# A hybrid SSD and attention layer in exact float32: parameters loaded behind the first block, x turned in the middle of a step, the last step in two banks

## The chip, the core and the metric

One core of a Trainium2 chip runs the whole layer. Its engines work in their own orders and wait for one another by semaphores: TensorE (PE in the rows; PEld are its weight loads) multiplies and transposes, VectorE (DVE) and ScalarE (ACT) do elementwise work, GpSimd (POOL) builds masks, and SyncE (SP) issues most of the loads. The metric is device time in microseconds of one execution, the median of several runs.

## The reference

```python
def hybrid_layer(x, norm_w, w_in, conv_w, conv_b, dt_bias, a_log, d_skip, ssd_norm_w, w_out):
    h = rmsnorm(x, norm_w)
    proj = h @ w_in                       # (256, 2048) @ (2048, 13344)
    z, xbc, dt_raw, q, k, v, g = jnp.split(proj, IN_SPLITS, axis=-1)
    xbc = jax.nn.silu(causal_depthwise_conv(xbc, conv_w, conv_b))
    xs, bm, cm = jnp.split(xbc, ...)
    y = ssd_chunked_scan(xs, softplus(dt_raw + dt_bias), -exp(a_log), bm, cm) + d_skip * xs
    y_ssd = group_rmsnorm(y * silu(z)) * ssd_norm_w
    y_sba = stick_breaking_attention(q, k, v) * silu(g)
    return x + concatenate([y_ssd, y_sba]) @ w_out    # (256, 4096) @ (4096, 2048)
```

A final RMSNorm with final_norm_w closes it. There are 256 tokens, all data are float32, and the time goes into the two large products.

## The kernel before

**Products.** Each large product is done in blocks of 256 or 512 columns of the weights, and a block in steps of two slices (kind "tok", the tokens' activations stand in the array) or four (kind "feat") of 128 rows of the weights. To keep float32 accuracy, weights and activations are each split into a high part that TensorE multiplies in one pass and a low part, and three products are added: high by high, high by low, low by high. `load` (L190) brings weights from HBM into one of four raw buffers; `cut` (L205) makes the parts, the high one as a cast on ScalarE (L218) and the low one as a subtraction on VectorE (L221); `product` (L224) issues the matmuls, for a "tok" step 12 of 512 columns (L235 to L237: two slices, two blocks of 128 tokens, three products).

**The first block, z0** (L282 to L306), is written out by hand for TensorE, ScalarE and VectorE. Here x arrives too: `load_x` (L352) loads 256 columns of x between the weight loads, on SP's queue; `prep_x` (L356) transposes them on TensorE (L363, four transposes a step), ScalarE scales each by norm_w into hT's high part (L366) and VectorE makes the low part (L367). The loop runs prep_x(s), then the cut of step s, then the product of step s-1. Eight matmuls of the identity (L296) go ahead, and norm_w itself comes through a small load and one transpose (`load_rows`, L100).

**Later blocks** run z1 to z3, c0, c1 (C and dt), b0, b1 (B), x0 to x3, then q, k, v, g of four head groups, and the output blocks o0 to o3. Each step's `advance` cuts two steps ahead. Between steps, `drain` (L143) takes side work from queues in order, up to a budget per step; an item's `lag` holds its queue back for so many steps after it. Side work here is the scaling of h, the convolutions (`conv`, L429), `decays` (L536), `b_tok` (L503, transposes B), `cb_block` (L556, products of C and B), the scan and the attention. Tile's scheduler places it in each engine's order.

**Parameters.** Convolution weights, biases, ssd_norm_w and three per-head vectors are loaded by GpSimd's queue at the start (L91 to L107) and two of them turned in `row_scale_bc` (L381).

**The end.** In o3 the second block of 128 tokens trails the first by three steps. `fin_last` (L837) adds the accumulator to x in two pieces of 256 columns (L846), squares each on ScalarE (L820) with a sum, forms 1/sqrt of the mean (L850 to L856), scales (L860 to L865) and stores eight pieces.

## Time and profile before

| what | value |
|---|---|
| median of 3 runs | 837.83 us (837.17 to 838.25) |
| the profiled execution | 837.44 us |
| its span in the trace | 835.7 us |
| TensorE busy | 821.0 us, 98% |
| VectorE, ScalarE busy | 520.3 us, 448.0 us |
| loaded from HBM | 152.43 MB, 185 GB/s over the span |

The rows further down are from this execution; their times count from the start of its span. A matmul's record is longer than its distance to the next one, since matmuls are pipelined, so distances between starts tell the rate, and short pauses hide in the records. In square brackets behind a row stand the idle time of its engine before it and what ended that.

### The profile page before, as it was taken

What the parts mean: (1) busy time and instruction counts of PE and PEld (TensorE: products, weight loads), DVE (VectorE), ACT (ScalarE), POOL (GpSimd) and SP (SyncE); (2) the same over time, 40 slices, a digit from 0 to 9 for tenths busy, and PEclk for the clock granted to TensorE, in tenths of its full rate; (3) what the DMA queues carried; (4) which work ended last, traced back from release to release, by engine and by line L of the source; (5) the groups of instructions that cost most, each with busy time, mean ns of one, the idle gap of its engine ahead of it and who ended that gap; (6) DMA issues with size and microseconds to landing.
All of it is one profiled execution on the core that took longest, in us unless ns stands there. A gap on an engine that the chain in (4) does not pass through costs nothing.

```text
span 835.7 us, 11182 instructions
## 1 busy us (share of the span) xinstructions
PE 821.0 (98%) x4341; PEld 701.0 (84%) x4341; DVE 520.3 (62%) x712; ACT 448.0 (54%) x671; POOL 63.7 (8%) x131
## 2 busy tenths in 40 slices
PE   8999999999999999999999999999999999999995
PEld 6888898888888888888888888888888888888884
DVE  4664959678896867676545654466545655455543
ACT  4754648785676756375444543455444544344433
POOL 2000000200101010022000400022000310000000
PEclk9999999999999999999999999999999999999998
DMA  8756477646656556464566446654565846555712
GB/s 289 274 199 201 136 213 219 204 151 202 197 157 199 170 187 199 119 186 152 154 199 202 151 152 201 201 164 150 191 187 179 338 152 191 184 185 197 250 52 100
DMA packets 113990, 155.29 MB, mean 186 GB/s; under 512 B 2836, under 2 KB 78704, under 8 KB 113552
## 3 DMA queue, kind: packets, MB, share of 16 engines
q1 hardware_dynamic: 112416, 149.18, 56.4%
q0 software_dynamic: 1520, 5.40, 2.0%
q8 instruction: 34, 0.56, 0.3%
q14 instruction: 20, 0.16, 0.1%
HBM read 152.43 MB, written 2.13 MB: 185 GB/s over the span
## 4 chain that ended last, share of the span: by engine, by line
PE 92%; DVE 3%; ACT 2%; issue 1%; DMA 1%; POOL 0%; SPq 0%; ACTq 0%; POOLq 0%
PE mm_g L241 7%; PE mm_k L241 7%; PE mm_o L235 7%; PE mm_o L236 7%; PE mm_o L237 7%; PE mm_q L241 6%; PE mm_x L241 5%; PE mm_k L244 4%; PE mm_g L244 4%; PE mm_v L237 3%; PE mm_v L235 3%; PE mm_v L236 3%; PE mm_z L235 3%; PE mm_z L236 3%; PE mm_z L237 3%; PE mm_q L244 3%
## 5 line engine op out<-in xcount | busy, mean ns | idle before, releaser
L221 DVE TENSOR_TENSOR lo_o<-raw_o,hi_o 128x1024 fp32r<-128x1024 f32 x64 | 78.1, 1224 | 74.3 <-ACT hi_o L218 74.2
L218 ACT CAST hi_o<-raw_o 128x1024 fp32r<-128x1024 f32 x64 | 67.1, 1053 | 93.5 <-PE mm_o L237 80.0
L241 PE MATMUL mm_q<-hT,hi_q 128*128 128x512 f32 x256 | 82.0, 401 | 0.0
L241 PE MATMUL mm_x<-hT,hi_x 128*128 128x512 f32 x256 | 81.7, 400 | 0.0
L241 PE MATMUL mm_k<-hT,hi_k 128*128 128x512 f32 x256 | 81.5, 400 | 0.0
L241 PE MATMUL mm_g<-hT,hi_g 128*128 128x512 f32 x256 | 80.9, 397 | 0.0
L221 DVE TENSOR_TENSOR lo_g<-raw_g,hi_g 128x1024 fp32r<-128x1024 f32 x32 | 39.2, 1226 | 45.4 <-ACT hi_g L218 43.8
L221 DVE TENSOR_TENSOR lo_v<-raw_v,hi_v 128x1024 fp32r<-128x1024 f32 x32 | 39.2, 1224 | 39.9 <-ACT hi_v L218 38.4
L218 ACT CAST hi_g<-raw_g 128x1024 fp32r<-128x1024 f32 x32 | 33.7, 1052 | 51.5 <-PE mm_g L241 31.1
L218 ACT CAST hi_v<-raw_v 128x1024 fp32r<-128x1024 f32 x32 | 33.6, 1050 | 45.9 <-PE mm_v L237 24.2
L244 PEld LDWEIGHTS mm_k<-hT,lo_k 128*128 128x128 f32 x256 | 48.1, 188 | 11.4
L244 PEld LDWEIGHTS mm_g<-hT,lo_g 128*128 128x128 f32 x256 | 48.1, 188 | 11.3
L244 PEld LDWEIGHTS mm_q<-hT,lo_q 128*128 128x128 f32 x256 | 48.1, 188 | 11.3
L244 PEld LDWEIGHTS mm_x<-hT,lo_x 128*128 128x128 f32 x256 | 48.0, 188 | 11.3
L221 DVE TENSOR_TENSOR lo_k<-raw_k,hi_k 128x1024 fp32r<-128x1024 f32 x32 | 39.2, 1224 | 27.7 <-ACT hi_k L218 27.7
L221 DVE TENSOR_TENSOR lo_z<-raw_z,hi_z 128x1024 fp32r<-128x1024 f32 (+1 forms) x33 | 39.2, 1192 | 25.1 <-ACT hi_z L218 24.9
L221 DVE TENSOR_TENSOR lo_q<-raw_q,hi_q 128x1024 fp32r<-128x1024 f32 x32 | 40.1, 1253 | 23.6 <-ACT hi_q L218 19.0
L218 ACT CAST hi_q<-raw_q 128x1024 fp32r<-128x1024 f32 x32 | 33.5, 1047 | 37.8 <-PE mm_q L241 17.6
L235 PE MATMUL mm_z<-hi_z,hT 128*128 128x512 f32 x128 | 50.6, 396 | 0.0
L218 ACT CAST hi_k<-raw_k 128x1024 fp32r<-128x1024 f32 x32 | 33.5, 1048 | 31.6 <-PE mm_k L241 23.5
L244 PE MATMUL mm_x<-hT,lo_x 128*128 128x256 f32 x256 | 50.5, 278 | 0.0
L244 PE MATMUL mm_q<-hT,lo_q 128*128 128x256 f32 x256 | 50.5, 278 | 0.0
(247 smaller groups left out, 1984.3 us busy)
## 6 DMA issues: line engine op xcount, KB each, us to landing
raw_o<-in_w_out_dram SPq DMA_DIRECT2D x32, 1024.0 KB, 5.2
raw_x<-in_w_in_dram SPq DMA_DIRECT2D x16, 1024.0 KB, 5.3
raw_q<-in_w_in_dram SPq DMA_DIRECT2D x16, 1024.0 KB, 5.3
raw_k<-in_w_in_dram SPq DMA_DIRECT2D x16, 1024.0 KB, 5.4
raw_v<-in_w_in_dram SPq DMA_DIRECT2D x16, 1024.0 KB, 5.0
raw_g<-in_w_in_dram SPq DMA_DIRECT2D x16, 1024.0 KB, 5.3
raw_z<-in_w_in_dram SPq DMA_DIRECT2D x12, 1024.0 KB, 5.1
raw_b<-in_w_in_dram SPq DMA_DIRECT2D x4, 1024.0 KB, 5.4
```

Source lines behind the costliest of these rows:

```text
L218: ins = ac.copy(hi[:, ks, :], src[:, ks, :])
L221: ve.tensor_tensor(out=lo[:, ks, :], in0=src[:, ks, :], in1=hi[:, ks, :].bitcast(F32), op=ALU.subtract)
L235: te.matmul(o, lhsT=ah[:, ts], rhs=hi[:, k2, :], start=first, stop=False)
L236: te.matmul(o, lhsT=ah[:, ts], rhs=lo[:, k2, :], start=False, stop=False)
L237: te.matmul(o, lhsT=al[:, ts], rhs=hi[:, k2, :], start=False, stop=last)
L241: te.matmul(acc[i], lhsT=hi[:, k2, i * P:(i + 1) * P], rhs=hT[:, k, :, :].rearrange("p a s -> p (a s)"), start=first, stop=False, skip_gro ...
L244: te.matmul(acc[i][:, 0:SEQ], lhsT=lo[:, k2, i * P:(i + 1) * P], rhs=hT_hi[:, k, :], start=False, stop=last, skip_group_check=True)
```

## The change

Five edits. The parameters are loaded by SP's queue behind the loads that the first block issues, and turned eight steps after the evacuation of z0 (`load_params`, `turn_params`); norm_w is loaded by ScalarE's queue. In the first block a step's product is done in two halves of one slice, and the transposes of the next step's x stand between them; x is scaled (`scale_x`) ahead of the next step's cut, and in the first cut slice by slice. There are six matmuls of the identity instead of eight. The lag behind B's last convolution is four instead of three, with two more behind the last `b_tok`; and the last step of the trailing token block in o3 goes into two banks of 256 columns (`product_end`), whose second square is done by VectorE.

```diff
-    nc.sync.dma_start(out=nw_rows, in_=norm_w[0].rearrange("(k p) -> k p", p=P))
+    ac.dma_start(out=nw_rows, in_=norm_w[0].rearrange("(k p) -> k p", p=P))
...
+    def load_params():
+        nc.sync.dma_start(out=par[0:4 * NT, :], in_=conv_w[0].rearrange("j (n p) -> (j n) p", p=P))
+        nc.sync.dma_start(out=par[4 * NT:5 * NT, :], in_=conv_b[0].rearrange("(n p) -> n p", p=P))
+        nc.sync.dma_start(out=sn_rows, in_=ssd_norm_w[0].rearrange("(k p) -> k p", p=P))
+        for i, src in enumerate((dt_bias, a_log, d_skip)):
+            nc.sync.dma_start(out=heads_bc[:, i, :], in_=src[0].partition_broadcast(P))
...
-        parts = [slice(0, width)] if b is not blocks[0] or s else [slice(i, i + 1) for i in range(width)]
+        parts = [slice(0, width)] if each is None else [slice(i, i + 1) for i in range(width)]
         for ks in parts:
+            if each is not None:
+                each(ks.start)
             ins = ac.copy(hi[:, ks, :], src[:, ks, :])
...
+    def product_end(b, s, i, halves):
+
+        hi, lo = cuts[b["name"], s]
+        ts, width = slice(i * P, (i + 1) * P), KS[b["kind"]]
+        for h, o in enumerate(halves):
+            ns = slice(h * 256, (h + 1) * 256)
+            for k2 in range(width):
+                ah, al = b["acts"](s * width + k2)
+                te.matmul(o[:, 0:256], lhsT=ah[:, ts], rhs=hi[:, k2, ns], start=k2 == 0, stop=False)
+                te.matmul(o[:, 0:256], lhsT=ah[:, ts], rhs=lo[:, k2, ns], start=False, stop=False)
+                te.matmul(o[:, 0:256], lhsT=al[:, ts], rhs=hi[:, k2, ns], start=False, stop=k2 == width - 1)
...
-            for i in range(8):
+            for i in range(6):
                 te.matmul(warm[:, 0:P], lhsT=ident, rhs=ident, start=True, stop=True)
             load_rows(nwT, nw_rows, KIN, "ps_nw")
-            for s in range(KIN // 2 + 1):
-                if s == 0:
-                    advance(1)
-                if s < KIN // 2:
-                    prep_x(s)
-                    advance(s + 1)
-                if s > 0:
-                    product(b, s - 1, acc, range(NB))
-                    done += 1
+            turn_x(0)
+            advance(1, each=lambda i: scale_x(i))
+
+            for s in range(KIN // 2):
+                product(b, s, acc, range(NB), (0,))
+                if s + 1 < KIN // 2:
+                    turn_x(s + 1)
+                    for i in range(2):
+                        scale_x(2 * s + 2 + i)
+                    advance(s + 2)
+                product(b, s, acc, range(NB), (1,))
+                done += 1
+            load_params()
...
-            push(main, (0, 1.1), evac)
+            push(main, (0, 1.1), evac, lag=8)
+            push(main, (0.5, 0), turn_params)
...
-                push(main, (1.2, 0.8), lambda g=g: conv(ut[:, g, :], BN + g, BT[:, g, :]), lag=g // 3 * 3)
+                push(main, (1.2, 0.8), lambda g=g: conv(ut[:, g, :], BN + g, BT[:, g, :]), lag=g // 3 * 4)
...
-                push(main, (0, 0.2), lambda g=g: b_tok(g))
+                push(main, (0, 0.2), lambda g=g: b_tok(g), lag=g // 3 * 2)
...
+            ve.tensor_tensor(out=y[:, b, 1536:2048], in0=acc[0], in1=y[:, b, 1536:2048], op=ALU.add)
+            for i in range(2):
+                c0 = 1536 + i * 256
+                yi = y[:, b, c0:c0 + 256]
+                ve.tensor_tensor(out=yi, in0=acc[1 + i][:, 0:256], in1=yi, op=ALU.add)
+                if i == 0:
+                    square_y(b, c0, 256, 3)
+                else:
+                    junk = pools["fin"].tile([P, 256], F32, name="junk_y")
+                    ve.scalar_tensor_tensor(out=junk, in0=yi, scalar=1.0 / D_MODEL, in1=yi, op0=ALU.mult,
+                                            op1=ALU.mult, accum_out=ysq[:, b, 4:5])
```

**TensorE in the first block.** `ps_x_6` and `ps_x_7` are the transposes of x for step 3, `hi_z0_2` and `lo_z0_2` the parts of step 2's weights, `hi_z0_3` and `lo_z0_3` those of step 3. Before:

```order
L237 MATMUL mm_z0_138<-hi_z0_1_199,hT_111 128x512
L363 MATMUL ps_x_6_243<-ident_72,xt_1_116 128x128 x2
L363 MATMUL ps_x_7_248<-ident_72,xt_1_116 128x128 x2
L235 MATMUL mm_z0_138<-hi_z0_2_227,hT_111 128x512
L236 MATMUL mm_z0_138<-lo_z0_2_228,hT_111 128x512
L237 MATMUL mm_z0_138<-hi_z0_2_227,hT_111 128x512
```

In the changed kernel:

```order
L255 MATMUL mm_z0_132<-hi_z0_2_225,hT_105 128x512
L391 MATMUL ps_x_6_241<-ident_72,xt_1_110 128x128 x2
L391 MATMUL ps_x_7_244<-ident_72,xt_1_110 128x128 x2
L253 MATMUL mm_z0_132<-hi_z0_2_225,hT_105 128x512
L254 MATMUL mm_z0_132<-lo_z0_2_226,hT_105 128x512
L255 MATMUL mm_z0_132<-hi_z0_2_225,hT_105 128x512
L253 MATMUL mm_z0_132<-hi_z0_2_225,hT_105 128x512
L254 MATMUL mm_z0_132<-lo_z0_2_226,hT_105 128x512
L255 MATMUL mm_z0_132<-hi_z0_2_225,hT_105 128x512
L253 MATMUL mm_z0_132<-hi_z0_3_251,hT_105 128x512
L254 MATMUL mm_z0_132<-lo_z0_3_252,hT_105 128x512
```

The transposes for step 3 stood ahead of all 12 matmuls of step 2, which were followed by the transposes for step 4 and then step 3; now they stand behind the first six of step 2, and step 3 follows the other six.

**ScalarE at the same place**, in the changed kernel:

```order
L396 ACTIVATE hT_105<-ps_x_6_241,nwT_90 128x256
L396 ACTIVATE hT_105<-ps_x_7_244,nwT_90 128x256
L222 CAST hi_z0_3_251<-raw_z0_1_139 128x1024
L396 ACTIVATE hT_105<-ps_x_8_267,nwT_90 128x256
L396 ACTIVATE hT_105<-ps_x_9_270,nwT_90 128x256
L222 CAST hi_z0_4_279<-raw_z0_2_161 128x1024
```

From step 1 on this is the order of before, two scaled copies of x and then the cast of the same step; VectorE's is the same with its two low parts and the subtraction. In step 0 the two casts stood ahead of the copies, and now each stands behind one.

**TensorE at B's side products.** `ps_bt` are the transposes of B, `ps_cb` the products of C and B, `mm_x0_1` the block x0_1. Before:

```order
L244 MATMUL mm_x0_0_1398<-hT_111,lo_x0_0_3_1434 128x256 x2
L505 MATMUL ps_bt_0_1495<-ident_72,BT_124 128x128
L505 MATMUL ps_bt_1_1498<-ident_72,BT_124 128x128
L505 MATMUL ps_bt_2_1501<-ident_72,BT_124 128x128
L505 MATMUL ps_bt_3_1504<-ident_72,BT_124 128x128
L241 MATMUL mm_x0_1_1523<-hT_111,hi_x0_1_0_1455 128x512 x2
```

In the changed kernel:

```order
L262 MATMUL mm_x0_1_1497<-hT_105,lo_x0_1_0_1454 128x256 x2
L538 MATMUL ps_bt_0_1520<-ident_72,BT_118 128x128
L538 MATMUL ps_bt_1_1523<-ident_72,BT_118 128x128
L538 MATMUL ps_bt_2_1526<-ident_72,BT_118 128x128
L538 MATMUL ps_bt_3_1529<-ident_72,BT_118 128x128
L259 MATMUL mm_x0_1_1497<-hT_105,hi_x0_1_1_1473 128x512 x2
```

The transposes of B moved from ahead of the first step of x0_1 to behind it; the products of C and B, which stood within that first step, now stand between its third and fourth.

## Rows read from the trace of the kernel before

**Rows 1.** Page, busy times: engine, busy us (share of the span), instructions

```profile
PE 821.0 (98%) x4341; PEld 701.0 (84%) x4341; DVE 520.3 (62%) x712; ACT 448.0 (54%) x671; POOL 63.7 (8%) x131
```

**Rows 2.** Windows: stretch, its us, each engine's busy us (instructions), clock, DMA, GB/s

```profile
0.00:20.00 20.00, 16.18 (x76) 13.22 (x77) 8.72 (x15) 9.52 (x17) 4.82 (x17) 1.00 0.89 285
...
20.00:40.00 20.00, 20.00 (x94) 16.27 (x94) 13.02 (x17) 15.14 (x31) 0.00 (x0) 1.00 0.84 299
...
800.00:836.00 36.00, 26.55 (x118) 21.66 (x116) 13.34 (x25) 12.51 (x21) 0.00 (x0) 0.90 0.16 59
```

**Rows 3.** TensorE's waits: who waited for whom, us in total, times, longest

```profile
PE ps_x L363 <- DMA xt<-in_x_dram: 2.3, 2, 1.3
```

**Rows 4.** Timeline, a step of z0: start, us, engine, line, op [idle before it]

```profile
15.69 0.60 PE L363 MATMUL ps_x<-ident,xt 128*128 128x128 f32 x4
...
16.05 0.48 PE L235 MATMUL mm_z<-hi_z,hT 128*128 128x512 f32 x1
...
16.11 0.84 ACT L366 ACTIVATE hT<-ps_x,nwT 128x256 fp32r<-128x256 f32 x2 [1.38 <-PE ps_x L363]
...
16.36 0.40 PE L236 MATMUL mm_z<-lo_z,hT 128*128 128x512 f32 x1
...
16.84 1.04 ACT L218 CAST hi_z<-raw_z 128x1024 fp32r<-128x1024 f32 x1
...
17.92 1.23 DVE L221 TENSOR_TENSOR lo_z<-raw_z,hi_z 128x1024 fp32r<-128x1024 f32 x1 [0.42 <-ACT hi_z L218]
...
18.91 0.60 PE L363 MATMUL ps_x<-ident,xt 128*128 128x128 f32 x4
...
19.58 0.40 PE L236 MATMUL mm_z<-lo_z,hT 128*128 128x512 f32 x1
```

**Rows 5.** Timeline: transposes of steps 2 and 7, first matmul of z1

```profile
12.45 0.63 PE L363 MATMUL ps_x<-ident,xt 128*128 128x128 f32 x4 [1.32 <-DMA xt<-in_x_dram]
...
28.51 0.60 PE L363 MATMUL ps_x<-ident,xt 128*128 128x128 f32 x4
...
34.63 0.39 PE L235 MATMUL mm_z<-hi_z,hT 128*128 128x512 f32 x1
```

**Rows 6.** Timeline: the start, on SP's queue, TensorE and ScalarE

```profile
0.81 0.39 SPq L88 DMA_DIRECT2D nw_rows<-in_norm_w_dram  x1
...
5.46 1.11 PE L363 MATMUL ps_x<-ident,xt 128*128 128x128 f32 x4
...
5.49 0.62 ACT L218 CAST hi_z<-raw_z 128x512 fp32r<-128x512 f32 x1 [3.20 <-DMA raw_z<-in_w_in_dram]
...
7.55 0.63 PE L363 MATMUL ps_x<-ident,xt 128*128 128x128 f32 x4 [0.97 <-DMA xt<-in_x_dram]
```

**Rows 7.** Windows of one us in the first block

```profile
9.00:10.00 1.00, 1.00 (x6) 0.82 (x5) 0.69 (x2) 0.82 (x1) 0.00 (x0) 1.00 1.16 185
...
13.00:14.00 1.00, 1.00 (x6) 0.81 (x5) 0.60 (x2) 1.00 (x3) 0.00 (x0) 1.00 1.06 385
```

**Rows 8.** Timeline: B's side products on TensorE

```profile
160.94 0.33 PE L505 MATMUL ps_bt<-ident,BT 128*128 128x128 f32 x1 [0.37 <-ACT BT L439]
...
163.75 2.05 PE L560 MATMUL ps_cb<-CT,BT 128*128 128x128 f32 x16 [0.61 <-ACT Btok L506]
```

**Rows 9.** Timeline: matmuls of 256 columns; VectorE behind the last matmul

```profile
400.32 0.40 PE L244 MATMUL mm_k<-hT,lo_k 128*128 128x256 f32 x2
...
400.55 0.63 PE L241 MATMUL mm_k<-hT,hi_k 128*128 128x512 f32 x2
...
825.31 0.75 DVE L860 SCALAR_TENSOR_TENSOR yfw<-yfw,sums 128x512 f32<-128x512 f32 x1
...
826.59 0.76 DVE L846 TENSOR_TENSOR yfw<-mm_o,yfw 128x256 f32<-128x256 f32 x2 [0.54 <-PE mm_o L237]
...
827.99 0.22 DVE L850 SCALAR_TENSOR_TENSOR sums<-ysq,sums 128x1 f32<-128x1 f32 x1 [0.64 <-ACT junk_o L820]
```

More of the change, by code (lines that the diff above doesn't have):

```diff
@@ L105, in hybrid_kernel @@
     heads_bc = const.tile([P, 3, HEADS], F32, name="heads_bc")
-    for i, src in enumerate((dt_bias, a_log, d_skip)):
-        gp.dma_start(out=heads_bc[:, i, :], in_=src[0].partition_broadcast(P))
+    def load_params():
[4 more added lines that the diff above has]
+            nc.sync.dma_start(out=heads_bc[:, i, :], in_=src[0].partition_broadcast(P))
     dtb_bc, alog_bc, dsk_bc = heads_bc[:, 0, :], heads_bc[:, 1, :], heads_bc[:, 2, :]
@@ L203, in load, with cut @@
             nc.sync.dma_start(out=raw, in_=src)
-    def cut(b, s):
+    def cut(b, s, each=None):
         n, name, width = b["n"], f"{b['name']}_{s}", KS[b["kind"]]
@@ L222, in cut, with product @@
         cuts[b["name"], s] = hi, lo
-    def product(b, s, acc, which):
+    def product_end(b, s, i, halves):
[8 more added lines that the diff above has]
+                te.matmul(o[:, 0:256], lhsT=al[:, ts], rhs=hi[:, k2, ns], start=False, stop=k2 == width - 1)
+    def product(b, s, acc, which, slices=None):
         nk, n, width = b["nk"], b["n"], KS[b["kind"]]
         hi, lo = cuts[b["name"], s]
-        for k2 in range(width):
+        for k2 in range(width) if slices is None else slices:
             k = s * width + k2
@@ L234, in product @@
                     o = acc[i][:, 0:n]
+                    if b["trail"] and i == 1:
+                        last = k == nk - 1 - width
                     te.matmul(o, lhsT=ah[:, ts], rhs=hi[:, k2, :], start=first, stop=False)
@@ L272, in advance_load, with advance @@
                 lead["load"] += 1
-        def advance(n_cut):
+        def advance(n_cut, each=None):
             while lead["cut"] < n_cut:
@@ L283, in advance @@
                 with (tc.high_priority() if b is not blocks[0] else ExitStack()):
-                    cut(b, s)
+                    cut(b, s, each)
                 lead["cut"] += 1
@@ L321, in run_blocks @@
                             b["finish"](acc, 0)
-                    if s >= trail:
+                    if s == ns + trail - 1:
+                        halves = [ps_mm.tile([P, 2, 512], F32, tag="mm", name=f"mm_{name}_1_{h}")[:, 0, :]
+                                  for h in range(2)]
+                        product_end(b, s - trail, 1, halves)
+                    elif s >= trail:
                         product(b, s - trail, acc, (1,))
@@ L331, in run_blocks @@
             else:
-                b["finish"](acc, 1)
+                b["finish"]([acc[1]] + halves, 1)
     r_tok = const.tile([P, NB], F32, name="r_tok")
@@ L364, in prep_x, with scale_x @@
                              in_=xt[q][:, b, h * 256 + j * P:h * 256 + (j + 1) * P], identity=ident)
-            src = pt[:, 0:SEQ]
-            ac.activation(hT_hi[:, k, :], src, AF.Copy, scale=nwT[:, k:k + 1])
-            ve.scalar_tensor_tensor(out=hT_lo[:, k, :], in0=src, scalar=nwT[:, k:k + 1],
-                                    in1=hT_hi[:, k, :].bitcast(F32), op0=ALU.mult, op1=ALU.subtract)
+            xT[k] = pt[:, 0:SEQ]
+    def scale_x(k):
+        ac.activation(hT_hi[:, k, :], xT[k], AF.Copy, scale=nwT[:, k:k + 1])
+        ve.scalar_tensor_tensor(out=hT_lo[:, k, :], in0=xT[k], scalar=nwT[:, k:k + 1],
+                                in1=hT_hi[:, k, :].bitcast(F32), op0=ALU.mult, op1=ALU.subtract)
     def square_x(i, b):
@@ L843, in fin_last @@
                 ve.tensor_scalar_add(sums[:, i, 0:1], sums[:, i, 0:1], EPS)
-        for i in range(2):
-            c0 = 1536 + i * 256
-            ve.tensor_tensor(out=y[:, b, c0:c0 + 256], in0=acc[b][:, i * 256:(i + 1) * 256],
-                             in1=y[:, b, c0:c0 + 256], op=ALU.add)
-            square_y(b, c0, 256, 3 + i)
+            for i in range(2):
+                c0 = 1536 + i * 256
+                ve.tensor_tensor(out=y[:, b, c0:c0 + 256], in0=acc[b][:, i * 256:(i + 1) * 256],
+                                 in1=y[:, b, c0:c0 + 256], op=ALU.add)
+                square_y(b, c0, 256, 3 + i)
+        else:
+            ve.tensor_tensor(out=y[:, b, 1536:2048], in0=acc[0], in1=y[:, b, 1536:2048], op=ALU.add)
+            for i in range(2):
+                c0 = 1536 + i * 256
+                yi = y[:, b, c0:c0 + 256]
+                ve.tensor_tensor(out=yi, in0=acc[1 + i][:, 0:256], in1=yi, op=ALU.add)
+                if i == 0:
+                    square_y(b, c0, 256, 3)
+                else:
+                    junk = pools["fin"].tile([P, 256], F32, name="junk_y")
+                    ve.scalar_tensor_tensor(out=junk, in0=yi, scalar=1.0 / D_MODEL, in1=yi, op0=ALU.mult,
+                                            op1=ALU.mult, accum_out=ysq[:, b, 4:5])
         v, sq, r, t = (sums[:, b, i:i + 1] for i in range(1, 5))
```

7 lines of the change are left out of this document (3 added, 4 removed).

## The prediction

> **What bounds the kernel now.** I read the page's busy table first: TensorE is busy for 98% of the span [rows 1], so the kernel is a stream of matmuls and a change pays by the idle time of TensorE that it takes away, and costs by what it adds. The windows say where that idle time is [rows 2]: 3.82 us of the first 20 us (20.00 less 16.18), none from 20 to 40 us, and 9.45 us of the last 36 us, nearly all of it behind the last matmul. The table of TensorE's waits names what ends the others: the transposes of x wait 2.3 us for loads [rows 3], and two side products of B wait for ScalarE [rows 8]. The end is TensorE's last matmul plus a serial tail on VectorE and ScalarE [rows 9].
>
> The timeline of one step of the first block, z0, is the row that matters most [rows 4]. In a step, four transposes of x at 15.69 release ScalarE at 16.11 (two scaled copies), then its cast of the weight slice at 16.84, then VectorE's subtraction at 17.92, which ends at 17.92 + 1.23 = 19.15. **So 3.46 us go by from the transposes to the low half of the weights.** The next transposes start at 18.91, 3.22 us after the first; the product that uses the low half starts that matmul at 19.58. The chain is just hidden, because in the kernel before one whole product of 12 matmuls and the next transposes stand between a step's transposes and the product that needs its cut.
>
> **The turn between a step's halves.** The order shows that this cover is halved. Now step s runs six matmuls, turns x for step s+1, runs six more, and then goes straight to step s+1, whose second matmul already needs the low half of the cut s+1. On ScalarE that cut still stands behind the two scaled copies of the freshly turned x, so it can't start earlier than the transposes allow. Call the start of the transposes for step s T(s). From T(s+1) on TensorE has 0.36 us of transposes (15.69 to 16.05) and six matmuls to do meanwhile. Eleven matmuls stand between 16.36 and 18.91 [rows 4], so one takes 0.23 us and six 1.4 us. The product asks for its low half about 2.0 us after T(s+1) (0.36 + 1.4, and one matmul of 0.23 that needs only the high half), and gets it after 3.46 + 0.05 us. The 0.05 us is my estimate of the hand-over, from the 0.04 us between the end of the cast and the subtraction in [rows 4] (16.84 + 1.04 to 17.92). TensorE then stands for 1.5 us in each step, and the steps form a loop: T(s+1), copies, cast, subtraction, the five matmuls of the half step that are left, T(s+2).
>
> Its period is 3.51 + 5 x 0.23 = 4.66 us. Before, from the transposes of step 2 at 12.45 to those of step 7 at 28.51 [rows 5], five periods took 16.06 us, or 3.21 each. **Five periods cost 5 x (4.66 - 3.21) = +7.25 us.** The end of the block is even: before, z1 starts at 34.63, 6.12 us behind the last transposes [rows 5]; now 3.51 us to the low half, 1.15 for five matmuls and 1.38 for the other six make 6.04 us (-0.1). Nothing later gives this back, since the stream behind is full already [rows 2].
>
> **The start.** The change also takes work from the front: the small DMA of nw_rows leaves SP's queue (0.39 us ahead of the first load of x [rows 6]), the six parameter loads leave the first 12 us, two of eight warm-up matmuls go, and the first cut is split between the two slices. In the window from 9 to 10 us the DMA engines moved 185 GB/s at a busy share over 1, and 385 GB/s from 13 to 14 [rows 7]: the small loads of parameters lie in the former, so the load of x that TensorE awaited at 12.45 comes earlier. But it doesn't decide any more. T(1) needs the second piece of x, whose landing released it at 7.55 [rows 6], now up to 0.45 us sooner; and it now stands behind six matmuls of step 0, which need the cast of the first weight piece and its subtraction. That cast began at 5.49 on the piece's landing [rows 6]; with about 0.6 us for it and 0.7 for the subtraction, and a scaled copy of 0.4 on either engine beside them, the low half is there at some 7.0, and five matmuls follow: I estimate T(1) at 8.2. T(2) can't come sooner than one loop behind: 8.2 + 4.66 = 12.9, against 12.45. So +0.4 us. Bounds: 7.1 + 4.66 = 11.8 (-0.7), and 13.8 (+1.4) if those five matmuls run at half rate and take another 1 us. That bound is from the rows on four transposes, 1.11 us at 5.46 and 0.63 at 7.55 [rows 6], although the window shows a granted clock of 1.00 throughout [rows 2]. [...]
>
> The six parameter loads now stand on SP behind the first load of z1, ahead of raw_z1_1. That one waits for a buffer that step 3 frees, so their issue (some 3 us at 0.4 to 0.6 each, as nw_rows' 0.39 [rows 6]) is covered; if the cover went, z1's third step would wait at most these 3 us, but that step's turn comes only near 48 us. Turning the parameters eight steps later costs nothing: their two transposes are the same, and the first convolution comes behind z3.
>
> **B's side products.** The four transposes of B move behind one step of x0_1, and the products with C two steps further. The waits were 0.37 us at 160.94 and 0.61 us at 163.75 [rows 8]; as matmul records overlap their successors by 0.17 us (0.40 long, 0.23 apart), each hides about that much more: 0.53 + 0.77 = 1.3 us. With one step of x0_1 more, four slices of 2 x 0.23 + 2 x 0.115 = 0.69 us, 2.8 us, the last copy of B is done by then, so **-1.3 us**; if a new wait took their place it would be 0. The mask multiplication that needs these products still waits for its exponentials. For the decays themselves the order shows no move at all: nothing.
>
> **The last step in two banks.** Six matmuls of 512 columns become twelve of 256. Two of 256 take 0.115 us each (400.32, and the next pair of rows at 400.55 [rows 9]), so 12 x 0.115 = 1.38 against 6 x 0.23: nothing. VectorE is busy with the other row block until 825.31 + 0.75 = 826.06. Then it adds 512 columns (about twice the 0.38 of a 256 add [rows 9]), two of 256, and squares one: about 0.7 + 0.76 + 0.4 = 1.9, to 827.9, where the sum that started at 827.99 can start [rows 9]. The half-way square on ScalarE lies beside it. -0.1 us, from -0.3 to +0.3.
>
> **Sum**: +7.25 - 0.1 + 0.4 - 1.3 - 0.1 = +6.2 us on the profiled execution's 837.44 us: 843.6. That execution lay 0.4 us under the median of the three runs, 837.83, so I put the median at 844.0.
>
> **Rivals.** (a) *The turn is free and the kernel faster.* If the cut of step s+1 came within 2.0 us of its transposes, steps would keep 3.21 us, T(7) would be at 8.2 + 6 x 3.21 = 27.5 and z1 at 27.5 + 0.36 + 12 x 0.23 + 1.4 = 32.0, 2.6 us before 34.63; with B and the tail -4.0: 833.8. For it: it takes away both waits for x. Against it: scaled copies, cast and subtraction alone are 0.73 + 1.08 + 1.23 us in [rows 4], more than 2.0, and the order leaves them in line. It decides only if the cast ran ahead of the copies. (b) *TensorE's clock falls in the pauses.* A pause of 1.5 us in every 4.7 leaves TensorE busy for about two thirds. At half rate six matmuls take 2.8 us, five 2.3, transposes 0.3 us more: the period would be 6.1 and the block 5 x 1.45 + 2.6 = 10 us longer still: 854. Against it: the profile grants 1.00 from 9 to 10 us and after [rows 7], in a stretch with pauses of 1 us and more [rows 3]. [...] (c) *The stall is partly refunded*, TensorE waiting less in B or the tail: within 0.2% of the time before; nothing in the windows from 20 us on leaves room for that.
>
> **How the numbers follow.** Forecast 0.83, (a) 0.07, (b) 0.07, (c) 0.03. The forecast's own bounds: front -0.7 to +1.4 in place of +0.4, B 0 to -1.3, tail +-0.3, 0.05 us a period: 842.0 to 847.0. The cases left out make up 0.17, so that is the range. A measurement of this kernel can tell about 0.2% (1.7 us) from no change; faster 0.07, same 0.03, slower 0.90.
>
> **What would show it.** In the trace of the changed kernel: idle time of TensorE of about 1.5 us in six or seven places before 43 us, each ended by VectorE's low half; transposes of x about 4.66 us apart; the first matmul of z1 near 42; no wait for B; the last sums near the same distance from the last matmul. If the transposes stand 3.2 us apart, my loop is wrong; if the matmuls themselves are 0.43 us apart, it was the clock.

## The result and the profile after

| | before | after |
|---|---|---|
| median | 837.52 us (836.69 to 838.25, 5 runs) | 846.77 us (845.78 to 848.05, 5 runs) |
| ratio | | 1.0114, interval 1.0099 to 1.0129 |
| profiled execution, its span | 837.44 us, 835.7 us | 848.04 us, 846.3 us |

The changed kernel is 1.1% slower: 9.25 us by the medians and 10.6 us between the two profiled executions, of which the one after lies at the upper end of its five runs. The forecast had +6.2 us. The direction and the loop in the first block hold; the term for B's side products does not. The ratio on the 837.83 us of the forecast gives 847.4 us, beyond the upper end, 847.

The page's busy table of the changed kernel (engine, busy us, share of the span, instructions) answers [rows 1]:

```profile
PE 825.3 (98%) x4343; PEld 701.2 (83%) x4343; DVE 520.5 (61%) x715; ACT 447.1 (53%) x669; POOL 61.7 (7%) x125
```

TensorE's share is still 98%, since a matmul's record (0.39 us long, with starts 0.23 us apart) covers short pauses. The windows (columns as in [rows 2]) tell more:

```profile
0.00:20.00 20.00, 15.81 (x62) 11.65 (x63) 6.58 (x12) 7.43 (x14) 1.59 (x11) 1.00 0.91 307
20.00:40.00 20.00, 15.96 (x69) 10.77 (x67) 9.25 (x14) 8.02 (x14) 0.00 (x0) 1.00 0.52 172
800.00:847.00 47.00, 37.05 (x170) 30.72 (x168) 18.91 (x31) 16.33 (x23) 0.00 (x0) 0.92 0.21 73
```

From 20 to 40 us TensorE was full before; now 4 us of it are idle and 69 records stand where 94 stood. The table of TensorE's waits, whole (who waits for whom, us in total, times, longest):

```profile
PE mm_z L254 <- DVE lo_z L225: 4.6, 6, 0.8
PE mm_z L253 <- ACT hi_z L222: 2.8, 9, 0.6
PE warm L314 <- POOL ident masks.py:199: 1.5, 1, 1.5
PE ps_xs L628 <- ACT cout L472: 1.3, 2, 0.9
PE ps_st L665 <- DVE mix_s_lo L714: 1.2, 1, 1.2
PE ps_ac L572 <- DVE da L504: 0.2, 1, 0.2
```

The wait for x [rows 3] and B's two waits [rows 8] are gone, as the change means. In their place stand the waits of z0's products for the two parts of the weights, and two that the forecast did not have: `ps_xs` (transposes of the first scan group's convolution output) and `ps_st` (the second scan group's state product, which waited 0.3 us before).

One step of z0 in the changed kernel, as in [rows 4] (start, us, engine, line, operation, idle time before it and what ended that):

```profile
28.59 0.60 PE L391 MATMUL ps_x<-ident,xt 128*128 128x128 f32 x4
...
29.01 0.84 ACT L396 ACTIVATE hT<-ps_x,nwT 128x256 fp32r<-128x256 f32 x2 [3.02 <-PE ps_x L391]
...
29.74 1.04 ACT L222 CAST hi_z<-raw_z 128x1024 fp32r<-128x1024 f32 x1
...
30.82 1.23 DVE L225 TENSOR_TENSOR lo_z<-raw_z,hi_z 128x1024 fp32r<-128x1024 f32 x1 [0.42 <-ACT hi_z L222]
30.84 0.50 PE L253 MATMUL mm_z<-hi_z,hT 128*128 128x512 f32 x1 [0.25 <-ACT hi_z L222]
...
32.10 0.50 PE L254 MATMUL mm_z<-lo_z,hT 128*128 128x512 f32 x1 [0.76 <-DVE lo_z L225]
32.43 0.39 PE L255 MATMUL mm_z<-hi_z,hT 128*128 128x512 f32 x1
...
33.34 0.60 PE L391 MATMUL ps_x<-ident,xt 128*128 128x128 f32 x4
```

Read it downwards: the transposes release the two scaled copies, these the cast, the cast the subtraction, and the product that needs the low part starts 32.10 - 28.59 = 3.51 us behind the transposes. Five matmuls later (1.24 us) come the next transposes. ScalarE's 3.02 us of idle time ahead of its copies says the same from the other side: the links of the loop run one after the other.

### The profile page after: what moved, and what is told of

It is laid out like the page before. It is cut to its first block, busy times and chain, and to the rows that moved or that the text cites. A ratio compares the mean times of both kernels' runs of the same rounds, so it can differ in the third digit from the quotient of the medians.

```text
span 846.3 us, 11184 instructions
## 1 busy us (share of the span) xinstructions
PE 825.3 (98%) x4343; PEld 701.2 (83%) x4343; DVE 520.5 (61%) x715; ACT 447.1 (53%) x669; POOL 61.7 (7%) x125
## 4 chain that ended last, share of the span: by engine, by line
PE 90%; DVE 3%; ACT 2%; DMA 2%; issue 2%; SPq 1%; POOL 0%; ACTq 0%; POOLq 0%; DVEq 0%
PE mm_g L259 7%; PE mm_k L259 7%; PE mm_o L253 7%; PE mm_o L255 7%; PE mm_o L254 7%; PE mm_q L259 6%; PE mm_x L259 6%; PE mm_k L262 4%; PE mm_g L262 3%; PE mm_v L253 3%; PE mm_v L254 3%; PE mm_v L255 3%; PE mm_q L262 3%; PE mm_x L262 3%; PE mm_z L254 3%; PE mm_z L255 3%
## 5 line engine op out<-in xcount | busy, mean ns | idle before, releaser
L254 PE MATMUL mm_z<-lo_z,hT 128*128 128x512 f32 x128 | 51.3, 401 | 4.6 <-DVE lo_z L225 4.6
L253 PE MATMUL mm_z<-hi_z,hT 128*128 128x512 f32 x128 | 52.3, 409 | 2.8 <-ACT hi_z L222 2.8
L225 DVE TENSOR_TENSOR lo_x<-raw_x,hi_x 128x1024 fp32r<-128x1024 f32 x32 | 39.1, 1223 | 18.5 <-ACT hi_x L222 16.8
L255 PE MATMUL mm_z<-hi_z,hT 128*128 128x512 f32 x128 | 50.5, 394 | 0.0
```

The costliest lines, as they stand in the source:

```text
L225: ve.tensor_tensor(out=lo[:, ks, :], in0=src[:, ks, :], in1=hi[:, ks, :].bitcast(F32), op=ALU.subtract)
L253: te.matmul(o, lhsT=ah[:, ts], rhs=hi[:, k2, :], start=first, stop=False)
L254: te.matmul(o, lhsT=ah[:, ts], rhs=lo[:, k2, :], start=False, stop=False)
L255: te.matmul(o, lhsT=al[:, ts], rhs=hi[:, k2, :], start=False, stop=last)
```

## The experiments

Each kernel ran in five rounds beside the kernel before; ratios are to the latter, whose median lay between 837.34 and 838.01 us. "T(s)" is the start of the transposes for step s.

| kernel | median | ratio (interval) | T(1), T(2), T(7) |
|---|---|---|---|
| before | 837.5 | | 7.55, 12.45, 28.51 |
| after | 846.77 | 1.0114 (1.0099 to 1.0129) | 9.39, 14.27, 38.12 |
| e1_loop_undone | 838.14 | 1.0003 (0.9993 to 1.0013) | 7.36, 13.36, 29.39 |
| e2_turn_alone | 846.10 | 1.0108 (1.0095 to 1.0121) | 8.91, 13.70, 37.49 |
| e3_cut_first | 837.47 | 0.9997 (0.9988 to 1.0005) | 9.39, 12.84, 28.87 |
| e7_cut_by_slice | 838.44 | 1.0005 (0.9994 to 1.0015) | 8.37, 11.81, 29.12 |
| e4_b_undone | 846.77 | 1.0112 (1.0097 to 1.0126) | 9.38, 14.47, 38.28 |
| e5_warm_8 | 847.38 | 1.0115 (1.0100 to 1.0130) | 8.86, 13.63, 37.46 |
| e10_fill | 846.49 | 1.0101 (1.0086 to 1.0116) | 8.34, 13.13, 36.96 |
| e6_tail_undone | 848.01 | 1.0119 (1.0105 to 1.0133) | 9.38, 14.46, 38.35 |
| e8_cut_first_rest_undone | 837.68 | 0.9993 (0.9984 to 1.0002) | 8.90, 13.23, 29.27 |
| e11_mended | 835.78 | 0.9976 (0.9967 to 0.9986) | 8.13, 11.58, 27.61 |
| e12_mended_pause | 835.61 | 0.9978 (0.9969 to 0.9987) | 8.37, 11.82, 27.97 |
| e13_after_pause | 847.07 | 1.0114 (1.0100 to 1.0128) | 9.39, 14.44, 38.30 |

### Is it the turn? Undone, and alone

**e1_loop_undone**: the changed kernel with the loop of before in z0.

```diff
-            for s in range(KIN // 2):
-                product(b, s, acc, range(NB), (0,))
-                if s + 1 < KIN // 2:
-                    turn_x(s + 1)
...
-                product(b, s, acc, range(NB), (1,))
...
+            for s in range(KIN // 2 + 1):
+                if s == 0:
+                    advance(1, each=lambda i: None)
+                if s < KIN // 2:
+                    prep_x(s)
+                    advance(s + 1)
+                if s > 0:
+                    product(b, s - 1, acc, range(NB))
...
```

> The changed kernel with the first block's loop as before (x turned ahead of a whole product), all other edits kept. Loop theory: the half-step turn makes up 9.4 us of the change (T(2) 1.8 us later, five periods of 4.77 in place of 3.21 us, the end 0.2 us shorter), so 846.8 - 9.4 = 837.4, and transposes 3.2 us apart again. Rival, B's side products gain 1.3 us as the prediction said: 836. Rival, the other edits cost by themselves (fewer warm-ups, parameters behind the block): 839 or more.

**e2_turn_alone**: the kernel before with the diff's loop of z0 (and `turn_x`, `scale_x`, the sliced first cut), and nothing else of the change.

```diff
-                    prep_x(s)
-                    advance(s + 1)
-                if s > 0:
-                    product(b, s - 1, acc, range(NB))
...
+                product(b, s, acc, range(NB), (0,))
+                if s + 1 < KIN // 2:
+                    turn_x(s + 1)
+                    for i in range(2):
+                        scale_x(2 * s + 2 + i)
+                    advance(s + 2)
+                product(b, s, acc, range(NB), (1,))
...
```

> The kernel before with the half-step turn alone; parameters, warm-ups, B's lags and the end as before. Loop theory: 837.5 + 8.5 to 9.4 = 846 to 847, TensorE waiting 1.0 us or more for VectorE's and ScalarE's parts in each step of the first block. Rival, the stall comes from the other edits at the start: below 842.

Undone, the time is that of before (838.14 us); alone, the turn costs 8.6 us (846.10). TensorE's waits in the kernel with the turn alone, the first and the fourth row:

```profile
PE mm_z L238 <- DVE lo_z L223: 4.8, 7, 0.8
...
PE ps_cb L569 <- ACT Btok L515: 0.6, 1, 0.6
```

The low part makes TensorE wait as in the changed kernel, and B's wait is there as before. So the turn is the loss, and the other four edits together come to nothing that the times tell. The executions of e1 spread widely, from 835.98 to 839.57 us, and the profiled one is the slowest of them; in it the first twelve matmuls start 0.43 us apart, and T(2) is at 13.36.

### Is it the chain behind the transposes, or any turn in mid-step?

**e3_cut_first**: the cut of the weights goes ahead of the scaled copies of x.

```diff
                     turn_x(s + 1)
+                    advance(s + 2)
                     for i in range(2):
                         scale_x(2 * s + 2 + i)
-                    advance(s + 2)
```

> The changed kernel with one exchange: the cut of the next step's weights is issued ahead of the scaled copies of the next step's x, so it no longer waits for the transposes. Loop theory: the chain from the transposes to the next half step shrinks to the scaled copies alone (about 1.4 us, under the 1.75 us of a half step), steps take 3.2 us again and the time is 834 to 837.5. Rival, TensorE is held by its clock or by loads there: it stays above 844.

**e7_cut_by_slice**: copy and cut alternate slice by slice in every step, not in step 0 alone.

```diff
                     turn_x(s + 1)
-                    for i in range(2):
-                        scale_x(2 * s + 2 + i)
-                    advance(s + 2)
+                    advance(s + 2, each=lambda i: scale_x(2 * s + 2 + i))
```

> The changed kernel, whose turn stays where it is, but in every step the scaled copy and the cut alternate slice by slice, as the change does in step 0 alone. Theory (the period is the chain from the transposes to the first low half that is asked for): that chain is now transposes 0.42, one copy 0.42, a cast of 512 columns 0.62 and a subtraction of 0.69, 2.15 us instead of 3.5, against 2.0 us of cover; the period falls from 4.77 to 3.3 us and the time to 838.0 (836.5 to 839.5). Rival (any turn between a step's halves costs, by the matmuls' order or the banks): the period stays at 4.5 or more and the time at 845 to 847.

Both leave the turn where the change put it, and both give back the whole loss: 837.47 and 838.44 us. Two following transposes of the one, then of the other:

```profile
22.46 0.60 PE L391 MATMUL ps_x<-ident,xt 128*128 128x128 f32 x4
25.68 0.60 PE L391 MATMUL ps_x<-ident,xt 128*128 128x128 f32 x4
```

```profile
22.20 0.60 PE L389 MATMUL ps_x<-ident,xt 128*128 128x128 f32 x4
25.66 0.60 PE L389 MATMUL ps_x<-ident,xt 128*128 128x128 f32 x4
```

The period falls from 4.77 us to 3.2 where the cut does not wait for the copies, and to 3.46 where the chain holds one copy and half a cut. That is the loop theory; a turn in the middle of a step costs nothing of itself that the times tell.

### The start

**e5_warm_8**: `range(6)` back to `range(8)` for the matmuls of the identity.

```diff
-            for i in range(6):
+            for i in range(8):
                 te.matmul(warm[:, 0:P], lhsT=ident, rhs=ident, start=True, stop=True)
```

> The changed kernel with eight matmuls of the identity instead of six. Theory (the first six matmuls of z0 stand 0.43 us apart since less work on TensorE goes ahead of them; with eight the turn alone had its transposes of step 1 at 8.91 and of step 2 at 13.70, against 9.39 and 14.27 with six): two more warm-ups end 0.84 us later, but the matmuls behind them run 0.23 apart, so the transposes of step 1 start at 8.9, all later ones 0.5 us sooner, and the time is 0.5 us less than the changed kernel's: 846.3 (845.5 to 847). Rival (the rate of those matmuls has nothing to do with the warm-ups, but with the parameters' loads or the split cut): they stay 0.43 apart, start 0.84 us later, and the time is 847.5.

**e10_fill**: six ahead, and two more between the transposes of step 0 and the first product.

```diff
             turn_x(0)
+            warm2 = side_ps("warm2")
+            for i in range(2):
+                te.matmul(warm2[:, 0:P], lhsT=ident, rhs=ident, start=True, stop=True)
             advance(1, each=lambda i: scale_x(i))
```

> The changed kernel with two more matmuls of the identity between the transposes of step 0 and the first product, in a stretch in which TensorE waits for ScalarE anyway; they delay nothing. Theory (the half rate of the first six matmuls comes from how little TensorE did before; the stretch of idleness of 0.6 us ahead of them adds to that): those six run 0.23 us apart, the transposes of step 1 start at 8.4 instead of 9.39, all later ones 0.9 us sooner, and the time is 845.9 (845.0 to 846.7). Rival (the rate is a matter of the single execution, since a kernel with the same start up to there showed 0.23 us): half rate may show again, with the transposes of step 1 at 9.4 and a time of 846.8, as the changed kernel's.

The end of the first six matmuls in the changed kernel:

```profile
8.11 0.63 PE L253 MATMUL mm_z<-hi_z,hT 128*128 128x512 f32 x1
8.54 0.63 PE L254 MATMUL mm_z<-lo_z,hT 128*128 128x512 f32 x1
8.96 0.63 PE L255 MATMUL mm_z<-hi_z,hT 128*128 128x512 f32 x1
9.39 0.71 PE L391 MATMUL ps_x<-ident,xt 128*128 128x128 f32 x4
```

and in the kernel with the two matmuls filled in:

```profile
8.11 0.39 PE L255 MATMUL mm_z<-hi_z,hT 128*128 128x512 f32 x1
8.34 0.60 PE L394 MATMUL ps_x<-ident,xt 128*128 128x128 f32 x4
```

Starts 0.43 us apart in the one, 0.23 in the other; with eight, 0.23 as well. In the traces that place the transposes of step 1 as theory has it (8.86 and 8.34 against 9.39), TensorE is ahead by 0.66 us and 1.16 us at T(7). The medians do not show it: 847.38 and 846.49 us against 846.77 are within what the runs of one kernel differ by. So only the traces speak for this term, with one execution of each kernel, and e5's forecast of 846.3 us missed. Nor is the number of warm-ups the whole cause: e7 has six and no fill, and its matmuls start 0.23 us apart too.

### B's lags

**e4_b_undone**: the lags of B's last convolution and of `b_tok` as before.

```diff
-   ... lambda g=g: conv(ut[:, g, :], BN + g, BT[:, g, :]), lag=g // 3 * 4)
+   ... lambda g=g: conv(ut[:, g, :], BN + g, BT[:, g, :]), lag=g // 3 * 3)
-                push(main, (0, 0.2), lambda g=g: b_tok(g), lag=g // 3 * 2)
+                push(main, (0, 0.2), lambda g=g: b_tok(g))
```

> The changed kernel with B's two lags as before. As predicted before the result, the lags save 1.3 us of waits, so without them 846.8 + 1.3 = 848.1. Theory after the trace: the wait only moves to the next place that needs ScalarE (the transposes of x's first group wait 1.3 us for cout, the state product 1.2 us for VectorE), so 846 to 847, and those two waits shrink to about 0 and 0.3 us while B's own waits return.

The time is that of the changed kernel, 846.77 us. Its waits have B's back:

```profile
PE ps_cb L593 <- ACT Btok L539: 0.6, 1, 0.6
PE ps_bt L538 <- ACT BT L472: 0.4, 1, 0.4
```

and `ps_xs` follows without a pause, as does the next product:

```profile
195.53 1.04 PE L628 MATMUL ps_xs<-ident,cout 128*128 128x128 f32 x8
196.33 0.71 PE L259 MATMUL mm_x<-hT,hi_x 128*128 128x512 f32 x2
```

With the change's lags the same stretch of the timeline reads

```profile
172.18 0.60 PE L538 MATMUL ps_bt<-ident,BT 128*128 128x128 f32 x4
178.20 1.95 PE L593 MATMUL ps_cb<-CT,BT 128*128 128x128 f32 x16
...
193.92 0.38 PE L628 MATMUL ps_xs<-ident,cout 128*128 128x128 f32 x2
194.69 0.33 PE L628 MATMUL ps_xs<-ident,cout 128*128 128x128 f32 x1 [0.38 <-ACT cout L472]
195.94 0.77 PE L628 MATMUL ps_xs<-ident,cout 128*128 128x128 f32 x5 [0.92 <-ACT cout L472]
196.46 0.71 PE L259 MATMUL mm_x<-hT,hi_x 128*128 128x512 f32 x2
```

B's 0.98 us are gone, and 1.30 us come at `ps_xs`, which waits for ScalarE's last convolution outputs. The split is clean: `ps_xs` waits 0.9 to 1.3 us in every profile with the new lags, and in none with the old ones. Counted from T(7), TensorE reaches `ps_xs` 1.45 us sooner with the new lags (193.92 - 38.12 = 155.80 against 195.53 - 38.28 = 157.25; 827 matmul records lie between in both), so B's waits were saved there. But it then takes 2.54 us instead of 0.80 to the next product. The convolution outputs come no sooner: the last starts on ScalarE at 195.47 us, 157.35 behind T(7), and with the old lags at 195.31, 157.03 behind it. ScalarE has no time to spare ahead of them. In the changed kernel it is busy for 19.92 of the 20 us from 170 to 190 (the fourth engine of the row):

```profile
170.00:190.00 20.00, 20.00 (x125) 17.74 (x124) 13.64 (x17) 19.92 (x41) 0.00 (x0) 1.00 0.52 158
```

From T(7) to the first state product it is 175.15 us in the changed kernel (38.12 to 213.27) and 174.86 in this one (38.28 to 213.14): in this pair the new lags cost 0.3 us. In e10, which has them too, it is 174.80.

### The end

**e6_tail_undone**: the last step and `fin_last` as before.

```diff
-                    if s == ns + trail - 1:
-                        halves = [...]; product_end(b, s - trail, 1, halves)
-                    elif s >= trail:
+                    if s >= trail:
                         product(b, s - trail, acc, (1,))
...
-                b["finish"]([acc[1]] + halves, 1)
+                b["finish"](acc, 1)
```

> The changed kernel with the last step and the end of the kernel before (one bank, the sum in two pieces of 256 columns, both squares on ScalarE). Theory: the end is worth 0.0 to 0.2 us, the end from the start of the last step goes from 10.84 us back to 10.67, and the time is 846.6 (845.5 to 847.5). Rival (two banks hide a part of the tail, as the forecast's -0.1 to -0.3 had it): 847.0 and an end of 10.9 to 11.1 us.

From the second state product to the end of the span it is 591.16 us in the changed kernel (255.14 to 846.3), 591.01 here (255.39 to 846.4), 590.99 before (244.71 to 835.7). The two banks cost 0.17 us where the forecast had -0.1. The time, 848.01 us, is above both expectations; this kernel's start is again the one with matmuls 0.43 us apart, and its 1.2 us over the changed kernel I can't tell from the spread of that kernel's own runs. VectorE in the changed kernel's tail:

```profile
837.17 0.75 DVE L888 TENSOR_TENSOR yfw<-mm_o,yfw 128x256 f32<-128x256 f32 x2
837.96 0.42 DVE L893 SCALAR_TENSOR_TENSOR junk_y<-yfw 128x256 f32<-128x256 f32 x1
838.31 0.08 DVE L893 DVE_READ_ACCUMULATOR junk_y<-yfw 128x1 f32 x1
838.50 0.22 DVE L896 SCALAR_TENSOR_TENSOR sums<-ysq,sums 128x1 f32<-128x1 f32 x1
```

From the first of the two adds to the sum it is 1.33 us, against 1.40 in [rows 9]: the squares on two engines gain a little. But the adds begin 1.71 us behind the start of the last step's matmuls (835.46), before 1.56 (825.03): twelve matmuls of 256 columns hold their end back by more than that.

### What could be kept

**e8_cut_first_rest_undone**: e3's loop, eight warm-ups, B's lags (as in e4) and the end (as in e6) as before.

```diff
-            for i in range(6):
+            for i in range(8):
...
                     turn_x(s + 1)
+                    advance(s + 2)
                     for i in range(2):
                         scale_x(2 * s + 2 + i)
-                    advance(s + 2)
...
```

> The turn between halves with the cut ahead of the scaled copies, eight warm-ups, B's lags and the end as in the kernel before; parameters loaded behind the first block as in the change. Theory: what is left of the change is the turn with its chain mended and the later parameters; the wait for x (2.3 us before) is partly gone, the transposes of step 7 come at 28.4 or sooner (28.87 with six warm-ups), and the time is 836.9 (836.0 to 837.6), level with the kernel before or 0.6 us less. Rival (the parameters or B's lags carry a gain that is lost here): 838 or more.

837.68 us, level with before: the forecast's 836.9 missed. T(2) comes at 13.23 and T(7) at 29.27, not 28.4: eight warm-ups start the first product 0.55 us later (6.91 against 6.36), and TensorE waits 0.4 us for the low part of step 1, which it gets at 11.80. By my estimate the cast of step 1 so began at 9.44 (11.80 less 0.05 of hand-over, 1.23 for the subtraction and 1.08 from cast to subtraction, as in e3); in e3 it began at 8.88, after standing for 1.69 us until its weights landed. At the second state product TensorE waits 1.2 us.

**e11_mended**: slice by slice in step 1, cut first from step 2 on, the two matmuls filled in (as in e10), B and the end as before (as in e4 and e6).

```diff
-                    for i in range(2):
-                        scale_x(2 * s + 2 + i)
-                    advance(s + 2)
+                    if s == 0:
+                        advance(2, each=lambda i: scale_x(2 + i))
+                    else:
+                        advance(s + 2)
+                        for i in range(2):
+                            scale_x(2 * s + 2 + i)
...
```

> The turn between halves with its chain mended: slice by slice in step 1, where the weights arrive late, and the cut ahead of the scaled copies from step 2 on; two more matmuls of the identity behind the transposes of step 0; B's lags and the end as in the kernel before. Theory: the transposes of step 1 start at 8.4, of step 2 at 11.8, later ones 3.2 us apart, those of step 7 at 27.9, where the kernel that only cuts first had 28.87; no wait for x or for low halves; time 836.5 (835.5 to 837.3), 0.1 to 0.2% under the kernel before. Rival (the loads of weights bound the block's first 20 us, or a wait of about 1 us turns up behind it, as the one that ends in the second scan group's state product): 837.5 to 838.

835.78 us, ratio 0.9976 (0.9967 to 0.9986): 0.24% faster than before, and faster than the changed kernel. T(7) in the timeline, and TensorE's longest wait behind z0:

```profile
27.61 0.60 PE L391 MATMUL ps_x<-ident,xt 128*128 128x128 f32 x4
```

```profile
PE ps_st L665 <- DVE mix_s_lo L714: 1.5, 1, 1.5
```

The first state product comes at 201.23 us, 2.46 us ahead of before (203.69), and the wait in the second takes half of that back (243.44 against 244.71).

**e12_mended_pause and e13_after_pause** look at that wait. GpSimd's select masks `seg` for one block of tokens of the second scan group, while VectorE multiplies `seg` of the other block by `cb`. In the changed kernel, VectorE's queue and GpSimd's:

```profile
234.82 1.22 DVE L655 TENSOR_TENSOR seg<-seg,cb 128x1024 f32<-128x1024 f32 x1
235.95 1.05 DVE L123 SCALAR_TENSOR_TENSOR gr<-rg_t,gr 128x2 f32<-128x2 f32 x1
```

```profile
234.94 2.06 POOL L643 TENSOR_SCALAR_AFFINE_SELECT seg<-seg 128x1024 f32<-128x1024 f32 x1 [4.03 <-DMA seg<-acT_d]
```

and before:

```profile
225.51 1.05 DVE L120 TENSOR_TENSOR rg_t<-rg_t,rg_h 128x2 f32<-128x2 f32 x1
226.48 1.21 DVE L622 TENSOR_TENSOR seg<-seg,cb 128x1024 f32<-128x1024 f32 x1
```

```profile
225.37 1.18 POOL L610 TENSOR_SCALAR_AFFINE_SELECT seg<-seg 128x1024 f32<-128x1024 f32 x1 [4.05 <-DMA seg<-acT_d]
```

Before, the select began first, and a tiny operation on VectorE (0.15 us elsewhere) took 1.05 us beside it; after, the multiplication began 0.12 us first, and the select took 2.06. ScalarE's exponentials, which wait for the select, then stood for 2.08 us instead of 1.21. In twelve profiles, all but the two of the test that follows, the wait at the second state product is 0.3 us or less where the select is short (1.1 to 1.2 us: before, e2, e4) and 1.2 to 1.5 where it is longer (1.5 to 2.2). The edit of both kernels:

```diff
             s = segs[b, g]
+            for i in range(2 if (b, g) == (0, 1) else 0):
+                ve.tensor_scalar_mul(s[:, GH - 1, 0:2], s[:, GH - 1, 0:2], 1.0)
             ve.tensor_tensor(out=s, in0=s, in1=cb[...], op=ALU.mult)
```

> The mended kernel with two tiny operations more on VectorE (128x2, times 1.0, in place) ahead of the multiplication of the second scan group's decays by cb; with them VectorE's order has that multiplication four small operations later. In the mended kernel GpSimd's select of that group's mask starts 0.08 us behind this multiplication (223.20 against 223.12) and takes 2.09 us; where it starts ahead, as in the kernel before, it takes 1.1 to 1.2. Theory (the two can't run at once; whichever starts first makes the other wait for its whole length, and ScalarE's exponentials, a cast, and TensorE's state product behind them stand for that): the select starts first and takes 1.1 us, TensorE's wait for the last low part of mix_s falls from 1.5 us to 0.5 or less, and the time from 835.8 to 834.9 (834.2 to 835.4). Rival (the length of the select is a consequence of something else, or VectorE's queue is the limit there): the wait stays at 1.2 us or more and the time at 835.8 or above.

> The changed kernel with the same two tiny operations on VectorE at the same place. Theory: the select, 2.06 us long and 0.12 us behind the multiplication in the changed kernel, starts first and takes 1.1 us; TensorE's wait for mix_s falls from 1.2 to 0.3 us, and the time by 0.9 us, to 845.7 (845.0 to 846.3). Rival: wait and time stay (1.2 us, 846.5 to 847).

In the mended kernel with the pause, select and state product:

```profile
223.11 1.33 POOL L643 TENSOR_SCALAR_AFFINE_SELECT seg<-seg 128x1024 f32<-128x1024 f32 x1 [3.88 <-DMA seg<-acT_d]
242.60 1.12 PE L667 MATMUL ps_st<-xds,Btok 128*128 128x512 f32 x2 [0.32 <-DVE mix_s_lo L716]
```

The select is short again and the wait falls from 1.52 to 0.32 us; in the changed kernel it falls from 1.18 to 0.72, with a select of 1.32. That the select is short when it starts well ahead of the multiplication (2.00 us in the mended kernel, 1.26 in the changed one), and that a large part of the wait goes with it, is shown. In e8 the select starts only 0.02 us ahead (224.73 against 224.75) and takes 2.19 us; how far ahead it has to be is not shown. That it is worth 0.9 us of time is not: 835.61 against 835.78 us and 847.07 against 846.77 are no differences, and both forecasts of the time missed, as did the 0.3 us of wait forecast for the changed kernel. By the spans of the profiled executions the mended kernel gained 0.8 us (833.7 against 834.5) and the changed one nothing (846.3 both). Whether the select came first in the other executions of these kernels too is not shown.

## Why the prediction was right where it was, and wrong in its size

The transposes of steps 2 and 7 in the changed kernel; the second matmul of z1 starts at 44.24 us (before at 34.86, one matmul behind the 34.63 of [rows 5]; z1's first one now slips in earlier):

```profile
14.27 0.60 PE L391 MATMUL ps_x<-ident,xt 128*128 128x128 f32 x4
...
38.12 0.60 PE L391 MATMUL ps_x<-ident,xt 128*128 128x128 f32 x4
```

and the second state product, in the changed kernel and before:

```profile
255.14 1.13 PE L665 MATMUL ps_st<-xds,Btok 128*128 128x512 f32 x2 [1.18 <-DVE mix_s_lo L714]
```

```profile
244.71 1.13 PE L632 MATMUL ps_st<-xds,Btok 128*128 128x512 f32 x2 [0.32 <-DVE mix_s_lo L681]
```

| step of the sum | forecast | profiled execution | how read |
|---|---|---|---|
| start, to T(2) | +0.4 (-0.7 to +1.4) | +1.8 | 14.27 against 12.45 |
| five periods | +7.25 | +7.8 | 38.12 - 14.27 = 23.85 against 16.06 |
| end of z0 | -0.1 | -0.2 | T(7) to z1's second matmul, 6.12 against 6.35 |
| B (0 to -1.3), and the scan | -1.3 | +1.05 | 255.14 - 44.24 = 210.90 against 209.85 |
| two banks and the end | -0.1 | +0.2 | 591.16 against 590.99 |
| sum | +6.2 | +10.6 | 846.3 - 835.7 |

**The loop: right.** The low part comes 3.51 us behind the transposes, the very figure of the forecast. The period is 4.77 and not 4.66 us, mostly since the matmul that has waited takes 0.33 us to the next one (32.10 to 32.43) instead of 0.23: 0.1 us each time, 0.5 of the 0.55 in five. The forecast took five equal matmuls behind a stall; it had allowed 0.05 us. It also expected one pause a step, for the low part; the rows show two, 0.25 us for the high part and 0.76 for the low, which leaves the length of the chain as it was. The cut ahead of the copies (e3) proves the step by taking it away.

**The start: the upper bound, and beyond.** T(1) at 8.2 us was right for a first product with matmuls 0.23 us apart: 8.34 with the two matmuls filled in, 8.37 in e7. In the profiled execution of the changed kernel the first six matmuls started 0.43 us apart from the third on, and T(1) was at 9.39; I had put that in the bound and not in the forecast. T(2) is then one period behind, 14.27 instead of the bound's 13.8: T(1) lies 0.2 us beyond the bound's 9.2, and this period takes 4.88 us instead of 4.66. With the matmuls of this start 0.23 us apart (e10) the account of the other terms is +0.7 to T(2), +7.8 for the periods, +0.5 from T(7) to the second state product, +0.2 at the end: 9.1 us, the difference of its spans (844.8 - 835.7). That is close to the 9.25 us of the medians. At what rate the other executions of the changed kernel began is not shown.

**B: the step that failed.** The term was -1.3 us, with 0 as its other end, "if a new wait took their place". The waits did go, and TensorE reached `ps_xs` 1.45 us sooner than with the old lags, about the size of the term. What failed is the path: the sum carried this gain through to the end, as if TensorE alone set the pace there. ScalarE, busy for 19.92 of 20 us there, set it as well; the convolution outputs came no sooner, and TensorE gave the gain back at `ps_xs`. That the gain comes and goes with the lags is shown by e4; that ScalarE's load is what holds the outputs is read from the rows, and no run took work off it. Up to the first state product the term measured +0.2 us (213.27 - 44.24 = 169.03 against 203.69 - 34.86 = 168.83), by the comparison with e4 +0.3, and in the time nothing (846.77 us with and without the lags). The other 0.85 us of the +1.05 in the table (41.87 us between the two state products against 41.02) are the second state product's wait, which the forecast did not have and which neither the lags nor the turn make by themselves: it is there in e8, which has the old lags, and in e1, which lacks the turn, and not in e2 and e4. It goes with the length of GpSimd's select beside VectorE's multiplication (1.1 to 1.2 us, or 1.5 to 2.2). Of the 4.4 us between the sum and the profiled execution, 2.35 lie in this line of the table, 1.4 at the start, 0.55 in the periods.

**The end: failed in sign, small.** +0.17 instead of -0.1, within its bounds of 0.3.

**The rivals.** (a) would have needed the cast ahead of the copies; e3, which does that, is the kernel that (a) described, and it is level with before (837.47), not at 833.8: its slow start leaves it 1.0 us ahead at the first state product (202.70 against 203.69), and the wait at the second takes most of that (244.57 against 244.71). (b), the clock in the pauses, did not happen: transposes stay 4.77 us apart to the end of z0 and the matmuls between them 0.23, and the window from 20 to 40 us, with its pauses of 0.25 and 0.76 us a step, grants a clock of 1.00. The clock reads 1.00 in the slow start too (each window of 1 us from 6 to 10 us of the changed kernel), so the forecast's test, matmuls 0.43 us apart as the sign of a slower clock, does not hold by these rows. (c) did not happen.

## What to carry to other kernels

When work is moved into the middle of a step, count the cover that is left for the slowest chain it feeds, and follow the engine orders, not the data: here x did not need to be copied before the weights were cast, but ScalarE's order said so, and one swap of two lines was worth 1.1%. The wait that the lags removed here (0.98 us) came back at the next consumer of the same engine's queue (1.30 us), where that engine was busy for 19.92 of 20 us; so read the busy time of the engine that was waited for before counting the wait as a gain. And where warm-up matmuls go, price the first matmuls at both rates seen here, 0.23 and 0.43 us.

## What the runs showed of the hardware

- **The rate of the first matmuls.** Where six warm-ups went ahead without a fill, the first matmuls started 0.43 us apart, from the third on, in six of seven profiles (after, e1, e3, e4, e6, e13; not e7, with the same start), and in none of the seven others (eight warm-ups, or six and two). In e1, where twelve stand in a row, they start 0.43 us apart from the second on. In the ten kernels whose windows were read (before, after, e1 to e8) the clock granted from 0 to 10 us is 1.00, so it is the distance of the starts that shows the rate. e7 says that it is not the number of warm-ups alone, nor the idle time ahead of the first matmul, which is 0.64 us in e7 and in the changed kernel; what else decides stays open.
- **GpSimd's select and VectorE's operations with two inputs were longer beside one another.** A 128x2 operation of VectorE with two inputs from SBUF took 1.05 us instead of 0.15 beside a select (before, at 225.51), and a select 2.06 us instead of 1.1 to 1.2 where a multiplication had begun 0.12 us ahead of it (after, at 234.94); in e4, where the select began 0.05 us ahead, it took 1.09 us and the multiplication 2.12 instead of 1.22. In e8 the select began 0.02 us ahead by the records, and yet it took 2.19 us and the multiplication 1.22. Between e4 and the changed kernel the two starts so differ by 0.17 us, and TensorE's table of waits has 1.2 us at the second state product in the changed kernel and none in e4.
